# Delta rule: transposes by VectorE's 32x32 turns and a DRAM buffer in place of TensorE's, in a generator of its own

## The chip, the core and the metric

One core of a Trainium2 chip runs the kernel. TensorE (PE, and PEld for its weight loads), VectorE (DVE), ScalarE (ACT), GpSimd (POOL) and SyncE (SP, which here only issues transfers) each work through their own queue in the order in which the program issued. The metric is the device time of one execution in microseconds; a profile's span runs from the first to the last instruction.

## What is computed

One layer of a hybrid decoder for 256 prompt rows and 32 sample rows (8 sequences of 4), width 2048, all in float32. The part that matters here is the gated delta rule with 8 heads of 128:

```python
qkv, new_gdn_buf = causal_depthwise_conv(jnp.concatenate([q, k, v], -1), gdn_buf, gdn_conv_w)
q, k, v = jnp.split(jax.nn.silu(qkv), 3, axis=-1)
qh = l2norm(q.reshape(hs)); kh = l2norm(k.reshape(hs)); vh = v.reshape(hs)
o, S = gated_delta_rule(qh, kh, vh, g, beta, S0)
o = o * lax.rsqrt(jnp.mean(o * o, -1, keepdims=True) + NORM_EPS) * gdn_norm_w
o = o * jax.nn.silu(z.reshape(hs))
y_b = o.reshape(Bsz, L, D_GDN) @ w_b_out
```

with, for each chunk of 64 rows, inside gated_delta_rule:

```python
M = jnp.where(strict, jnp.einsum('nbhid,nbhjd->nbhij', kb, kc) * decay, 0.0)
T = lax.linalg.triangular_solve(eye + M, eye, left_side=True, lower=True, unit_diagonal=True)
u = T @ (vc * bc);  w = T @ (kb * jnp.exp(gcum)[..., None])
...
v_new = u_c - w_c @ S
o = qd @ S + a_c @ v_new
S = S * jnp.exp(gl)[..., None] + jnp.einsum('bhcd,bhce->bhde', kd, v_new)
```

Around it stand the projections: x @ w_in (11280 columns), w_a_out, w_b_out, w_o, and the two feed-forward products with 8192 hidden columns.

## The kernel before

**The main stream.** Every weight is cut into blocks of 512 KB. A block is loaded on SP's queue (`load`, tile raw), split into two float32r halves, hi on ScalarE (`split_hi`) and lo on VectorE (`split_lo`), and used by 24 matmuls (`matmuls`: hi by x's high part, hi by its low part, lo by its high part). The loop at the end of `hybrid_kernel` takes block i in step i; in it the engines get, in this order: `split_hi(i + 3)`, one part of the side work, `split_lo(i + 3)`, the evacuations that are due, the 24 matmuls of block i, and `load(i + 7)`. raw, hi and lo have four buffers each.

**The evacuations.** Four blocks make a group of 256 columns; for keys, queries and values of a half of the heads (two groups each) its convolution comes one step after the group (`conv_evac`, f: two copies and a product on ScalarE, small copies on POOL, three L143 instructions on VectorE), the second 128 columns one step later, and the Silu two steps later. The first half's groups are blocks 0 to 23 (keys, queries, values), the second half's 24 to 47; then come the groups of the short convolution (48 to 95) and z (96 to 111), whose evacuation multiplies into ao, so the delta rule's output has to lie there by then.

**The side work.** `side()` is a generator: gates, then `gdn(0)` and `gdn(1)`, each a half of the heads. A part up to the next `yield` is issued in each step, ahead of the step's matmuls on TensorE's queue. gdn starts in step 20 for the first half. The delta rule needs rows where the projection gives columns (heads' channels on the partitions), and takes them by TensorE transposes against the identity: kq (L958), the sample's kqs (L973, L974, L980), v (L1219) and the output (L1291). For the sample rows four matmuls against a widened Us (L1176) give v_new in another arrangement. `T` and its inverse are built by steps of 8, 16 and 32 (L1084), `states_of` multiplies the sample's keys and queries into S0 (L1072), and a chain over four chunks c does p1 (L1231), p2 (L1243), p3 (L1251) and p4 (L1254). Its first instruction on v scales v by nr, out of PSUM.

**The sample's generator.** `sample()` is a second generator (`aux`); one part of it is issued in each step after the side work. Its first part has sp1 (L1139 to L1142) and Es, its third and fourth the decays of S0 on POOL (L1126), and further ones spread v3 over vm on POOL (L1192), multiply it (pn, L1203) and add to S0.

In the profile, L143 and L140 are the helpers `stt` and `tt`, so one line stands for many operations of VectorE; the tile names tell them apart (lo, w, v, E).

Of the kernel before, what the change touches and what calls it, by code (L numbers as in the profile page):

```python
# [9 lines left out]
F32 = mybir.dt.float32  # L10
# [93 lines left out]
def hybrid_kernel(ctx: ExitStack, tc: tile.TileContext, A):  # L104
# [11 lines left out]
    gp = pool("gp", 4, space=PSUM)  # L116

# [798 lines left out]
    def four(ap):  # L916
        return ap.rearrange("p (h t) -> p h t", h=4).unsqueeze(2).to_broadcast([P, 4, 4, 32])

    def gdn(G):
# [4 lines left out]
        S0 = pl.tile([P, 4, 8, P], F32, tag="S0", name=nm("S0"))  # L924
        for hh in range(4):
            gps.dma_start(S0[:, hh], A["state_gdn"][0, :, 4 * G + hh].rearrange("b d e -> d b e"))

        def T(shape, tag):
            return pl.tile(shape, F32, tag=tag, name=nm(tag))
# [8 lines left out]
        sqr = T([P, 1024], "vmh")  # L938
        rep4 = sqr[:, 512:1024]
        junk = sqr[:, 192:320]  # L940
        wide = rep4.rearrange("p (h q t) -> p h q t", h=4, q=4)
# [5 lines left out]
        gl = T([P, 4, 2, 64], "gl")  # L947
        ss = T([P, 22], "ss")
        red = T([P, 4, 4], "red")
        kdec = T([P, 4, 2, P], "kdec")  # L950
        kst, qst = (kqs[:, u].rearrange("p h b t -> p (h b t)") for u in range(2))
        rows = (slice(0, 64), slice(64, 128))

        for c in range(4):
            kt = gtile()
            kv = kt.rearrange("p (h c) -> p h c", h=4)
            for hh in range(4):
                pe.transpose(kv[:, hh, :], kq[:, hh, c].rearrange("p s x -> p (s x)"), ident)  # L958
            s2 = sqr[:, 512 * (c % 2):512 * (c % 2) + 512].rearrange("p (h c) -> p h c", h=4)
            act.activation(s2, kv, AF.Square)  # L960
            for par in range(2):
                act.copy(kdec[rows[par], c], kv[rows[par], par::2, :])
            dve.tensor_reduce(out=red[:, c, :], in_=s2, axis=mybir.AxisListType.X, op=ADD)
            if c % 2:
# [3 lines left out]
        ssv = ss[:, 0:16].rearrange("p (a c r) -> p a c r", a=2, c=4)  # L968
        for par in range(2):
            act.copy(ssv[rows[par], 0], red[rows[par], :, par::2])  # L970
            act.copy(ssv[rows[par], 1], red[rows[par], :, 1 - par::2])
        sp2 = gtile()
        pe.transpose(sp2[:, 0:128], kst, ident)  # L973
        pe.transpose(sp2[:, 128:256], qst, ident)  # L974

        gps.tensor_copy(wide, four(kst))
        yield
        ktr = gtile()
        for hh in range(4):
            pe.transpose(ktr[:, hh * P:hh * P + P], rep4[:, hh * P:hh * P + P], ident)  # L980
        kr = T([P, 4, P], "kr")
        for u in range(2):
            act.activation(junk, sp2[:, u * P:u * P + P], AF.Square, accum_out=ss[:, 16 + u:17 + u])
        act.copy(kr, ktr.rearrange("p (h d) -> p h d", h=4))
        act.activation(sqr[:, 0:512], ktr, AF.Square)
        dve.tensor_reduce(out=ss[:, 18:22], in_=sqr[:, 0:512].rearrange("p (h d) -> p h d", h=4),
                          axis=mybir.AxisListType.X, op=ADD)
# [6 lines left out]
        yield  # L994
# [26 lines left out]
        kdf = kdec.rearrange("p c r x -> p (c r) x")  # L1021
        tt(kdf, kdf, bc(qc(kdr), P), MUL)
# [21 lines left out]

        Uf, Tf = U.rearrange("p q c -> p (q c)"), Tm.rearrange("p q c -> p (q c)")
# [41 lines left out]
        spread_kq(0)  # L1087
# [48 lines left out]
        def sample():  # L1136
# [32 lines left out]
            act.copy(wide, four(Us))  # L1169
# [4 lines left out]
            vtr = gtile()  # L1174
            for hh in range(4):
                pe.matmul(vtr[:, hh * P:hh * P + P], rep4[:, hh * P:hh * P + P], vs, start=True, stop=True)  # L1176
            vr = sqr[:, 0:512].rearrange("p (h d) -> p h d", h=4)
            tt(vr, vtr.rearrange("p (h d) -> p h d", h=4), bc(rsc[:, 1], P), MUL)
            v3 = pl.tile([P, 4, P], F32R, tag="U", name=nm("v3"))
            lows(v3, vr, 1)  # L1180
            yield
            po = gtile()
# [29 lines left out]
        while cur[0] < mark["kqv_end", G] + 3:  # L1212
            yield
# [241 lines left out]
```

## Time and profile before

| what | us |
|---|---|
| three runs, median | 1707.81 |
| lowest and highest of them | 1706.11, 2056.02 |
| the profiled execution, span from first to last instruction | 1703.4 |
| TensorE busy in it | 1688.5 |
| VectorE, ScalarE, GpSimd busy | 1007.2, 734.1, 133.8 |

No time of the profiled execution other than its span is given; the median of the runs is 4.4 above that span. In the profile's groups, a row has line, engine, operation, output and inputs with their shapes, the count, and then busy time in us, mean of one in ns, and the idle time of the engine just before with what ended it. In the chain and the timeline a row starts with the start and the duration in us, counted from the span's start. Matmuls overlap, so the distance from one start to the next is the price of one, not its duration.

### The profile page before, as it was taken

How to read it: one execution, taken by the hardware profiler on the slowest of the kernel's cores; microseconds unless marked ns; L12 is line 12 of the kernel's file. 1: busy time of each engine (PE TensorE's matmuls, PEld its weight loads, DVE VectorE, ACT ScalarE, POOL GpSimd, SP SyncE). 2: the span in 40 equal slices, each digit the busy share in tenths (PEclk: the TensorE clock that was granted, in tenths of full speed). 3: DMA queues.
4: the chain of work that ended last, by engine and by line, in shares of the span. 5: the costliest groups of instructions: out<-in, count | busy, mean ns of one | idle time of the engine just before them, and what ended most of it. 6: DMA issues, size and time to landing. Idle time of an engine off the chain costs nothing.

```text
span 1703.4 us, 31106 instructions
## 1 busy us (share of the span) xinstructions
PE 1688.5 (99%) x13063; PEld 1668.7 (98%) x13063; DVE 1007.2 (59%) x1296; ACT 734.1 (43%) x1067; POOL 133.8 (8%) x223
## 2 busy tenths in 40 slices
PE   9999999999999999999999999999999999999997
PEld 7999999999999999999999999999999999999997
DVE  5577876758544444456778844566445654466565
ACT  4675626333543333334445533444334433344442
POOL 2232412023300000000010000000000000000000
PEclk9999999999999999999999999999999999999999
DMA  8464456435555555555565555555555555555552
GB/s 244 140 194 139 123 175 200 150 115 180 162 170 169 166 162 170 163 164 165 158 190 174 165 170 161 164 170 162 167 168 161 163 171 162 164 167 164 162 162 80
DMA packets 275097, 279.18 MB, mean 164 GB/s; under 512 B 13131, under 2 KB 270092, under 8 KB 274952
## 3 DMA queue, kind: packets, MB, share of 16 engines
q1 hardware_dynamic: 270414, 265.95, 51.3%
q0 software_dynamic: 4256, 11.12, 2.3%
q8 instruction: 102, 1.67, 0.4%
q14 instruction: 37, 0.30, 0.1%
q10 hardware_dynamic: 288, 0.13, 0.0%
HBM read 269.68 MB, written 7.48 MB: 163 GB/s over the span
## 4 chain that ended last, share of the span: by engine, by line
PE 98%; DVE 1%; DMA 0%; POOL 0%; issue 0%; SPq 0%; ACT 0%; POOLq 0%; ACTq 0%
PE acc L206 31%; PE acc L208 31%; PE acc L207 31%; PE g L1084 1%; DMA xr<-in_x_prompt_dram 0%; PE g L1072 0%; PE g L1231 0%; PE g L1251 0%; PE g L831 0%; DVE w L143 0%; PE g L1254 0%; PE g L1203 0%; PE g L1243 0%; PE g L608 0%; PE g L798 0%; PE g L958 0%
## 5 line engine op out<-in xcount | busy, mean ns | idle before, releaser
L140 DVE TENSOR_TENSOR lo<-raw,hi 128x1024 fp32r<-128x1024 f32 (+2 forms) x502 | 614.0, 1226 | 556.2 <-ACT hi L179 553.7
L179 ACT CAST hi<-raw 128x1024 fp32r<-128x1024 f32 (+1 forms) x498 | 517.6, 1041 | 765.0 <-PE acc L207 707.7
L206 PE MATMUL acc<-xh,hi 128*128 128x288 f32 x1408 | 422.9, 300 | 0.0
L208 PE MATMUL acc<-xh,lo 128*128 128x288 f32 x1408 | 416.7, 296 | 0.0
L207 PE MATMUL acc<-xl,hi 128*128 128x288 f32 x1408 | 416.5, 296 | 0.0
L206 PE MATMUL acc<-dh,hi 128*128 128x290 f32 x1024 | 303.9, 297 | 0.0
L207 PE MATMUL acc<-dl,hi 128*128 128x290 f32 x1024 | 303.3, 296 | 0.0
L208 PE MATMUL acc<-dh,lo 128*128 128x290 f32 x1024 | 302.7, 296 | 0.0
L206 PE MATMUL acc<-hh,hi 128*128 128x288 f32 x1024 | 302.3, 295 | 0.0
L208 PE MATMUL acc<-hh,lo 128*128 128x288 f32 x1024 | 302.3, 295 | 0.0
L207 PE MATMUL acc<-hl,hi 128*128 128x288 f32 x1024 | 302.3, 295 | 0.0
L206 PEld LDWEIGHTS acc<-xh,hi 128*128 128x128 f32 x1408 | 265.4, 189 | 2.6 <-issue 0.7
L207 PEld LDWEIGHTS acc<-xl,hi 128*128 128x128 f32 x1408 | 265.8, 189 | 0.5
L208 PEld LDWEIGHTS acc<-xh,lo 128*128 128x128 f32 x1408 | 265.6, 189 | 0.0
L206 PEld LDWEIGHTS acc<-dh,hi 128*128 128x128 f32 x1024 | 193.6, 189 | 0.1
L208 PEld LDWEIGHTS acc<-dh,lo 128*128 128x128 f32 x1024 | 193.3, 189 | 0.0
L207 PEld LDWEIGHTS acc<-dl,hi 128*128 128x128 f32 x1024 | 193.3, 189 | 0.1
L207 PEld LDWEIGHTS acc<-hl,hi 128*128 128x128 f32 x1024 | 192.5, 188 | 0.0
L208 PEld LDWEIGHTS acc<-hh,lo 128*128 128x128 f32 x1024 | 192.3, 188 | 0.0
L206 PEld LDWEIGHTS acc<-hh,hi 128*128 128x128 f32 x1024 | 192.1, 188 | 0.0
L207 PE MATMUL acc<-ml,hi 128*128 128x288 f32 x256 | 75.6, 295 | 0.0
L208 PE MATMUL acc<-mh,lo 128*128 128x288 f32 x256 | 75.6, 295 | 0.0
(404 smaller groups left out, 1620.0 us busy)
## 6 DMA issues: line engine op xcount, KB each, us to landing
raw<-in_w_in_dram SPq DMA_DIRECT2D x176, 512.0 KB, 3.5
raw<-in_w_up_dram SPq DMA_DIRECT2D x128, 512.0 KB, 3.9
raw<-in_w_down_dram SPq DMA_DIRECT2D x128, 512.0 KB, 3.7
raw<-in_w_o_dram SPq DMA_DIRECT2D x32, 512.0 KB, 3.7
raw<-in_w_a_out_dram SPq DMA_DIRECT2D x16, 512.0 KB, 3.7
raw<-in_w_b_out_dram SPq DMA_DIRECT2D x16, 512.0 KB, 3.6
S<-in_state_gdn_dram POOLq DMA_DIRECT2D x8, 512.0 KB, 7.8
out_dram<-S POOLq DMA_DIRECT2D x8, 512.0 KB, 4.9
```

The costliest lines, as they stand in the source:

```text
L140: dve.tensor_tensor(out=out, in0=a, in1=b, op=op)
L179: act.copy(his[i][:, k:k + step], raw[i][:, k:k + step])
L206: pe.matmul(o, wh, xh_, start=st, stop=False)
L207: pe.matmul(o, wh, xl_, start=False, stop=False)
L208: pe.matmul(o, wl, xh_, start=False, stop=en)
L1084: pe.matmul(out[r, q * 64:q * 64 + 64], a[r, q, :], b[r, q, :], start=True, stop=True)
```

## The change

It touches five things.

1. A pool in DRAM (`dp`) and turns of 32x32 blocks on VectorE take the place of TensorE's transposes. Each is a `dve.transpose`, a write of its 32-row bands to DRAM and a read back in the other arrangement, all on SP's queue: keys and queries (dk), the sample's (ds), v (dv) and the output (do, read straight into ao).
2. What had been the start of gdn is a generator of its own, `prepare(G)`: it is put on a new list `ahead` in step 19 for the first half, and at the end of the first half's `sample()` for the second. One part of it is issued in a step, after `side()` and only when `aux` is empty. gdn(G) starts when prepare(G) has put its tiles into `front`.
3. v is turned and loaded inside gdn, long before its use, and the scaling by nr is one VectorE instruction from SBUF to SBUF, directly ahead of the first p2.
4. The sample's four matmuls against the widened Us are gone: pv goes to DRAM (dx) and comes back as v4. The spread of v3 starts in the same part as v3.
5. S0 shares its tile with the turned keys and queries, so its loads on POOL come after mx; in the chain over chunks every p2 has two parts ahead of its p3, and p3 one ahead of the next p1, in both halves.

```diff
+    def prepare(G):
...
+        for hh in range(4):
+            dve.transpose(out=tk[:, :, hh % 2, :, hh // 2],
+                          in_=kq[:, hh].rearrange("p c s x -> p c (s x)").rearrange("p c (j b) -> p j c b", j=4))
+            if hh == 1:
+                dve.transpose(out=ts.rearrange("p u h x -> p (u h x)"), in_=kqs.rearrange("p u h b t -> p (u h b t)"))
+            if hh == 1:
+                yield
+        ds = dp.tile([8, 32, P], F32, tag="ds", name=nm("ds"))
+        for i in range(4):
+            sp.dma_start(ds[:, :, rows32(i)].rearrange("h b x -> b h x"), ts[rows32(i)].rearrange("p u h x -> p (u h) x"))
+        yield
+        dk = dp.tile([P, 4, 2, 256], F32, tag="dk", name=nm("dk"))
+        for i in range(4):
+            sp.dma_start(dk[:, i].rearrange("(j b) a t -> b j (a t)", j=4),
+                         tk[rows32(i)].rearrange("p j a c r x -> p j (a c r x)"))
+        sp.dma_start(spk, ds.rearrange("(u h) b d -> (h b) u d", u=2))
...
+        yield
+        for a in range(2):
+            r = rows[a]
+            sp.dma_start(kT[r].rearrange("p i c r x -> p i (c r x)"), dk[r, :, a])
+            sp.dma_start(qT[r].rearrange("p i c r x -> p i (c r x)"), dk[r, :, 1 - a])
+        for q in range(4):
+            sp.dma_start(kr[rows32(q)], ds[0:4].rearrange("h b d -> b h d"))
+        yield
...
+        yield
+        yield
+        for u, t in enumerate((kT, qT)):
...
+        yield
...
+        front[G] = (sqr, ss, kT, tv, spk, kr, glx)
     def gdn(G):
...
-            for hh in range(4):
-                pe.transpose(kv[:, hh, :], kq[:, hh, c].rearrange("p s x -> p (s x)"), ident)
...
-        pe.transpose(sp2[:, 0:128], kst, ident)
-        pe.transpose(sp2[:, 128:256], qst, ident)
...
-            pe.transpose(ktr[:, hh * P:hh * P + P], rep4[:, hh * P:hh * P + P], ident)
...
+        while cur[0] < mark["kqv_end", G] + 3:
+            yield
+        for r in range(2):
+            dve.transpose(out=tv[:, :, :, r],
+                          in_=vf[:, r].rearrange("p c a x -> p c (a x)").rearrange("p c (j b) -> p j c b", j=4))
+        yield
...
+            sp.dma_start(dv[:, i].rearrange("(j b) t -> b j t", j=4),
+                         tv[rows32(i)].rearrange("p j c r x -> p j (c r x)"))
+        yield
+        sp.dma_start(v.rearrange("p i c r x -> p i (c r x)"), dv.rearrange("p i t -> p (i t)").rearrange("p (i t) -> p i t", i=4))
...
         act.copy(mx[:, 0], Xf)
         gps.tensor_tensor(out=mx[:, 1], in0=Xf, in1=mx[:, 0], op=SUB)
+        S0 = T([P, 4, 8, P], "S0")
+        for hh in range(4):
+            gps.dma_start(S0[:, hh], A["state_gdn"][0, :, 4 * G + hh].rearrange("b d e -> d b e"))
         yield
+        spread_kq(0)
         yield
...
             pe.matmul(pv_[:, 0:P], Us, vs, start=True, stop=True)
+            act.copy(Xs, pv_[:, 0:P])
             act.mul(vns, pv_[:, 0:P], sc[:, 1:2])
-            for hh in range(4):
-                pe.matmul(vtr[:, hh * P:hh * P + P], rep4[:, hh * P:hh * P + P], vs, start=True, stop=True)
...
+            yield
+            sp.dma_start(dx, Xs)
...
             done.append(1)
+            yield
+            for q in range(4):
+                sp.dma_start(v4[rows32(q)], dx.rearrange("(h b) d -> b h d", h=4))
+            yield
+            yield
+            vr = sqr[:, 0:512].rearrange("p (h d) -> p h d", h=4)
+            tt(vr, v4, bc(rsc[:, 1], P), MUL)
+            v3 = pl.tile([P, 4, P], F32R, tag="U", name=nm("v3"))
+            lows(v3, vr, 1)
...
             store(3)
+            if G == 0:
+                ahead.append(prepare(1))
...
         aux.append(sample())
-        v = T([P, 4, 2, P], "v")
-        for u in range(2):
-            vt = gtile()
-            for w in range(4):
-                pe.transpose(vt[:, w * P:(w + 1) * P], vf[:, w % 2, 2 * u + w // 2].rearrange("p a x -> p (a x)"), ident)
-            tt(v[:, 2 * u:2 * u + 2].rearrange("p c r x -> p (c r) x"), vt.rearrange("p (q x) -> p q x", q=4),
-               bc(nr[:, 4 * u:4 * u + 4], P), MUL)
-        yield
+        yield
+        vq = v.rearrange("p i c r x -> p i (c r) x")
+        tt(vq, vq, bc(bmid(nr[:, 0:8], 4), 32), MUL)
...
             p2 = gtile()
             for p in range(2):
-                pe.matmul(p2[:, p * P:(p + 1) * P], U128[:, 2 * c + p, :], v[:, c, p, :], start=True, stop=True)
+                pe.matmul(ix(p2[:, p * P:(p + 1) * P]), U128[:, 2 * c + p, :], v[:, :, c, p], start=True, stop=True)
...
-            if c == 0 or G == 0:
-                yield
+            yield
...
-            if G == 0:
-                yield
...
+        to = T([P, 4, 2, 4, 32], "kdec")
+        for r in range(2):
+            dve.transpose(out=to[:, :, r], in_=o[:, :, r].rearrange("p c (j b) -> p j c b", j=4))
+        yield
+        do = dp.tile([2, 2, P, 2, 4, 32], F32, tag="do", name=nm("do"))
+        for i in range(4):
+            sp.dma_start(do[1 - i // 2, i % 2].rearrange("(j b) r c x -> b j (r c x)", j=4),
+                         to[rows32(i)].rearrange("p j r c x -> p j (r c x)"))
+        yield
+        for a in range(2):
+            for r in range(2):
+                t0 = gd["ao"][:, 1, 4 * G + a + 2 * r, 0:NP_].rearrange("p (c n x) -> p n c x", c=4, n=2)
+                for n in range(2):
+                    sp.dma_start(t0[:, n], do[a, n, :, r])
         yield
...
         for G in range(2):
-            while cur[0] < mark["kqv", G] + 20 or aux:
+            while G not in front or aux:
                 yield
...
+                if i == mark["kqv", 0] + 19:
+                    ahead.append(prepare(0))
                 next(sgen, None)
                 if aux and next(aux[0], aux) is aux:
                     aux.pop(0)
+                if ahead and not aux and next(ahead[0], ahead) is ahead:
+                    ahead.pop(0)
```

More of the change, by code (lines that the diff above doesn't have):

```diff
@@ L913, in gates, with rows32, T @@
         yield
-    def four(ap):
-        return ap.rearrange("p (h t) -> p h t", h=4).unsqueeze(2).to_broadcast([P, 4, 4, 32])
-    def gdn(G):
+    def rows32(n):
+        return slice(32 * n, 32 * n + 32)
+    def T(shape, tag, bufs=1):
+        return gd["pool"].tile(shape, F32, tag=tag, name=nm(tag), bufs=bufs)
+    rows = (slice(0, 64), slice(64, 128))
+    front = {}
+    def prepare(G):
         pl = gd["pool"]
-        hs = slice(4 * G, 4 * G + 4)
         pr = slice(2 * G, 2 * G + 2)
-        kq, kqs, vf, vfs = gd["kq", G], gd["kqs", G], gd["v", G], gd["vs", G]
-        S0 = pl.tile([P, 4, 8, P], F32, tag="S0", name=nm("S0"))
-        for hh in range(4):
-            gps.dma_start(S0[:, hh], A["state_gdn"][0, :, 4 * G + hh].rearrange("b d e -> d b e"))
-        def T(shape, tag):
-            return pl.tile(shape, F32, tag=tag, name=nm(tag))
-        def qc(ap):
-            return ap.rearrange("p c r -> p (c r)")
-        b4 = T([P, 1152], "b4")
-        Es, Ts, Xs, nMs, aTs, Us, vs, vns, junk2 = (b4[:, P * u:P * u + P] for u in range(9))
-        kqm = b4.rearrange("p (a x) -> p a x", a=2)
[L938 to L941, printed above, removed]
-        U128 = T([P, 8, P], "U128")
-        aT = T([P, 8, P], "aT")
-        gps.memset(kqm, 0.0)
-        for z in (U128, aT):
-            gps.memset(z, 0.0)
[L947 to L956, printed above, removed]
-            for hh in range(4):
[L958 to L964, printed above, removed]
-                yield
@@ L994, in gdn, with qc @@
         yield
+        for u, t in enumerate((kT, qT)):
+            s2 = sqr.rearrange("p (q i x) -> p i q x", q=8, i=4)
+            act.activation(s2, t.rearrange("p i c r x -> p i (c r) x"), AF.Square)
+            dve.tensor_reduce(out=ss[:, 8 * u:8 * u + 8], in_=sqr.rearrange("p (q d) -> p q d", q=8),
+                              axis=mybir.AxisListType.X, op=ADD)
+        yield
+        for u in range(2):
+            act.activation(junk, spk[:, u], AF.Square, accum_out=ss[:, 16 + u:17 + u])
+        act.activation(sqr[:, 0:512], kr.rearrange("p h d -> p (h d)"), AF.Square)
+        dve.tensor_reduce(out=ss[:, 18:22], in_=sqr[:, 0:512].rearrange("p (h d) -> p h d", h=4),
+                          axis=mybir.AxisListType.X, op=ADD)
+        front[G] = (sqr, ss, kT, tv, spk, kr, glx)
+    def gdn(G):
+        pl = gd["pool"]
+        hs = slice(4 * G, 4 * G + 4)
+        pr = slice(2 * G, 2 * G + 2)
+        kq, kqs, vf, vfs = gd["kq", G], gd["kqs", G], gd["v", G], gd["vs", G]
+        sqr, ss, kT, tv, spk, kr, glx = front[G]
+        v4 = sqr[:, 512:1024].rearrange("p (h d) -> p h d", h=4)
+        def qc(ap):
+            return ap.rearrange("p c r -> p (c r)")
+        b4 = T([P, 1152], "b4")
+        Es, Ts, Xs, nMs, aTs, Us, vs, vns, junk2 = (b4[:, P * u:P * u + P] for u in range(9))
+        kqm = b4.rearrange("p (a x) -> p a x", a=2)
+        U128 = T([P, 8, P], "U128")
+        aT = T([P, 8, P], "aT")
+        gps.memset(kqm, 0.0)
+        for z in (U128, aT):
+            gps.memset(z, 0.0)
+        kdec = T([P, 4, 2, P], "kdec")
+        kst, qst = (kqs[:, u].rearrange("p h b t -> p (h b t)") for u in range(2))
         gr = gtile()
```

67 lines of the change are left out of this document (29 added, 38 removed).

## The prediction

> **What bounds the kernel now.** I read the page's first part (who is busy), its fourth part (the chain that ended last), then who waited for whom, then the chain in order of time around the delta rule.
>
> ```profile
> PE 1688.5 (99%) x13063; PEld 1668.7 (98%) x13063; DVE 1007.2 (59%) x1296; ACT 734.1 (43%) x1067; POOL 133.8 (8%) x223
> ...
> PE 98%; DVE 1%; DMA 0%; POOL 0%; issue 0%; SPq 0%; ACT 0%; POOLq 0%; ACTq 0%
> ...
> L179 ACT CAST hi<-raw 128x1024 fp32r<-128x1024 f32 (+1 forms) x498 | 517.6, 1041 | 765.0 <-PE acc L207 707.7
> ```
>
> TensorE is the bound: 99% busy, 98% of the chain. ScalarE's copy of a weight block waits for TensorE (707.7 of 765.0 us), not for a transfer, so the weight stream runs ahead. So only two things move the time: instructions taken off TensorE's queue, and waits that come or go in that queue. The only long wait inside the span, and its weaker twin in the second half of the heads, are these (waits view, then chain):
>
> ```profile
> PE g L1203 <- DVE E L143: 3.0, 1, 3.0
> ```
> ```profile
> 405.38 0.61 DVE E L143 x2
> ```
>
> **What comes off TensorE.** The chain in order of time gives each kind of removed work; the row of L973 (L974 is equal) is from the groups by form:
>
> ```profile
> 92.99 0.87 PE g L958 x8
> 97.06 0.87 PE g L958 x8
> 104.53 0.44 PE g L980 x4
> ...
> 180.11 0.87 PE g L1219 x8
> 184.95 0.61 PE g L1243 x4
> ...
> 201.15 0.89 PE g L1176 x8
> ...
> 271.72 0.87 PE g L1291 x8
> ...
> 366.19 0.87 PE g L1219 x8
> 371.03 0.44 PE g L1243 x4
> ```
> ```profile
> L973 PE MATMUL g<-cf,kqs 128*128 128x128 f32 x2 | 0.5, 272 | 0.0
> ```
>
> A step without other work is 97.06 - 92.99 - 0.87 = 3.20 us, so the 0.87 is fully added to its step. Per half of the heads the change drops 16 key/query transposes (2 x 0.87), 8 of v (0.87), 8 of the output (0.87), 4 of L980 (0.44), 2 of L973/L974 (2 x 0.87/8 = 0.22) and the 8 passes of L1176 (0.89): 5.03. Both halves: **-10.1 us**. The matmuls that stay (L1243, L1251, L1254) read v in four runs of 32 columns instead of one of 128; no row shows such a read, I take the same price; bounds: nothing, and a doubling of L1243's 0.44 in its 8 uses (+3.5).
>
> **What VectorE and the rest pay.** Turning adds, per half, 8 instructions of 128x512 and one of half that:
>
> ```profile
> L1114 DVE STREAM_TRANSPOSE xt<-U x4: 711/712/712, 155.9 to 352.8; 128x512 f32<-128x512 f32 x4
> ```
> ```profile
> 92.70:439.40 346.70, 343.63 (x3054) 335.69 (x3053) 253.15 (x407) 175.88 (x338) 82.95 (x121) 1.00 0.52 156
> ```
>
> That is 8 x 0.71 + 0.4 = 6.1 us. The reductions before (five a half) become three of like total. VectorE is 253.15 of 346.70 us busy here (73%), so 6 us in some 130 us find room; ScalarE loses the copies out of PSUM. By themselves these cost nothing: a block's halves are ready three steps (9.6 us) ahead. If that cover goes, the price is where TensorE waits for a VectorE result in the same step; that is the main item below.
>
> **The transfers.** Weights and the new round trips share SP's queue:
>
> ```profile
> raw<-in_w_in_dram SPq DMA_DIRECT2D x176, 512.0 KB, 3.5
> ...
> ao<-in_w_in_dram SPq DMA_DIRECT2D x1, 128.0 KB, 5.9
> ```
>
> SP waits for each turn on VectorE, and for each write before its read; the weight load of that step is queued behind. Write and read are one step apart (3.2 us) against some 3.5 us landing, so SP loses a microsecond or two. The worst burst is the eight loads of a half's output into ao: 8 x 128 x 4 = 4096 pieces of 128 B. The nearest row moved 2048 pieces of 64 B in 5.9 us, so 4096 take at most 11.8. Load i+7 leaves about 2.5 us into step i (after hi 1.04 and lo 1.2) and must be split by step i+7: 22.4 - 2.5 - 3.5 - 2.3 = 14 us of room. Cost taken: zero; bounds 0 and 5 (burst, issues and a late write together). The Trainium skill ("DMA: Bandwidth & Descriptors", Specifications) says that pieces below 512 B fall short of line rate through a read-modify-write; this speaks against the change, and the 5.9 us row is in its favour. By that rule the burst is longer than its bytes ask for, which the 11.8 us from the row already allows.
>
> Every other step that moves (S0's loads on POOL from the start of gdn to after mx, six steps ahead of states_of; v's turn; dx and v4 with two steps between load and use) has at least two steps (6.4 us) before its user: zero. The second half's front starts when the first half's sample is stored, and its first turn waits for that store on VectorE; TensorE needs nothing of it for 8 steps: zero.
>
> **The new wait.** Before, v was scaled by nr one step ahead of the first matmul on it (p2, L1243). Now the scaling is issued in the same step as p2, directly ahead of it, behind all that VectorE has from the step before. Counting the yields: prepare(0) runs in steps 19 to 26, gdn(0) starts at 27, U128 and the first part of sample are step 45, the scaling and p2 step 46. Before, they were steps 42 and 43. The same VectorE and ScalarE work, both halves:
>
> ```profile
> 367.04 1.24 ACT L1121 COPY U<-U 64x512 f32<-64x512 f32 x2
> ...
> 368.55 0.35 ACT L1145 ACTIVATE b<-g,nr 128x128 f32<-128x128 f32 x1
> ```
> ```profile
> 368.93 0.35 DVE L143 SCALAR_TENSOR_TENSOR b<-g,sc,b 128x128 f32<-128x128 f32 x1 [0.63 <-ACT b L1145]
> ...
> 370.10 0.31 DVE L1151 STREAM_TRANSPOSE b<-b 128x128 f32<-128x128 f32 x1
> 370.34 1.18 DVE L140 TENSOR_TENSOR lo<-raw,hi 128x1024 fp32r<-128x1024 f32 x1
> ```
> ```profile
> L140 DVE TENSOR_TENSOR kdec<-kdec,kdr 128x1024 f32<-128x1024 f32 x2 | 2.4, 1215 | 0.0
> ```
>
> Second half: VectorE is through with the step's lo at 371.5; the scaling (128x1024, like kdec's, 1.22) ends at 372.7. TensorE reaches p2 at 371.03 less the 0.87 of the removed transposes, 370.16. **+2.6 us** of wait.
>
> First half: the same, plus a table load on ScalarE, plus a convolution piece (three instructions of L143 for the value columns, blocks 40 to 43, due in steps 44 and 45), and POOL's four decays of S0. These are issued in steps 47 and 48, but POOL has nothing queued ahead of them after step 45's small copies, so it runs them early, as it did before:
>
> ```profile
> 182.22 1.28 ACT L1144 ACT_TABLE_LOAD   x1
> ```
> ```profile
> 174.01 1.70 DVE L143 SCALAR_TENSOR_TENSOR w<-w,hw 128x312 f32<-128x312 f32 x3 [0.61 <-ACT w L270]
> ...
> 179.24 4.89 DVE L143 SCALAR_TENSOR_TENSOR w<-w,hw 128x312 f32<-128x312 f32 x3
> 184.04 1.28 DVE L140 TENSOR_TENSOR v<-g,nr 128x512 f32<-128x512 f32 x2
> ```
> ```profile
> 178.19 5.01 POOL L1126 TENSOR_TENSOR S<-S,gexp 128x1024 f32<-128x1024 f32 x2
> ```
> ```profile
> 345.30 3.79 POOL L1126 TENSOR_TENSOR S<-S,gexp 128x1024 f32<-128x1024 f32 x2
> ```
>
> Beside two decays the three took 4.89 us instead of 1.70, and the decays 5.01 instead of 3.79: the two engines take turns. Set the step's side work at 180.11 as in the row: TensorE reaches p2 at 184.95 - 0.87 = 184.1. ScalarE's table load ends 183.5, Exp and the copy of vs 184.1, VectorE's chain takes to 185.6 (as 368.9 to 370.4). Without POOL: lo 1.2, three of L143 1.7, scaling 1.2, end 189.7: a wait of 5.6. With POOL: the four decays start about 184.9, after the piece's copies, and now nothing stands between the second and the third; 4 x 1.9 = 7.6 of decays and 4.1 of VectorE in turn end at 196.6: a wait of 12.5. Before, only two decays came at this place. I take **+12.5**, nearest to the 179.24 row, bounds 5.6 and 13.
>
> The Trainium skill ("SBUF — State Buffer", Who interferes with whom) has it as an exclusive lock: a VectorE instruction with two SBUF inputs and a POOL instruction that reads SBUF block each other for a whole instruction. If instead both only slowed (factor 4.89/1.70 for L143, less for the others), the scaling would end about two microseconds earlier, a wait near 10.5; the rows (5.01 and 4.89 interleaved) are nearer to turns.
>
> **Old waits.** The 3.0 us came from POOL's spread meeting the last value pieces (steps 49, 50). The spread now comes in step 54, where no such piece runs: -3.0. The 0.61 is a PSUM buffer that the sample's product wants while p3 still holds it; p3 and the first product now meet in both halves (steps 56 and 97): 2 x 0.61 - 0.61 = +0.6; bounds 0 and 3.
>
> **Sum.** -10.1 - 3.0 + 12.5 + 2.6 + 0.6 = +2.6 us on a span of 1703.4: 1706.0. The runs' median 1707.81 is 4.4 above the span (lowest 1706.11: 2.7), start and end around it; I keep that 4.4 and get **1710 us**. Bounds of the pieces: 5.6 in place of 12.5 gives 1703; all upper ends (13, 3, 5, 3.5) give 1722.
>
> **Rivals.** *Faster, the waits are hidden:* VectorE reaches the scaling before TensorE reaches p2. Then -10.1 - 3.0 + 0.6 = -12.5: 1695. For it: in the 184.04 row v was ready just in time though VectorE was late. Against: there it had a step (4 us) more. It decides if VectorE is less than half a microsecond behind; a partial form with POOL out of the way (5.6 + 2.6) gives 1703. *Slower, the output burst starves the weights:* if 128 B pieces take 11.8 us and land only after the 14 us of room, TensorE stands in both halves; from 14 us on each further one costs two. At 20 us: 2.6 + 12 = +15, 1722. Against: the 5.9 us row is an upper bound already. *The change does not take TensorE's time off* (strided reads doubling): +3.5, 1714.
>
> **Chances.** Both waits about as worked out (1706 to 1715): 0.55; partly hidden (1699 to 1706): 0.17; hidden (under 1699): 0.13; burst or strided reads (over 1715): 0.15. The range leaves out half of the last two: 1697 to 1720; the likeliest alone is 1706 to 1715. Two per cent (34 us) is about what a measurement of this kernel can tell from none: faster would need three times the removed work (0.01), slower 45 us of new stalls (0.02), the rest within (0.97).
>
> **What would show it.** Right: no L958, L980, L1176, L1219, L1291 kinds left on TensorE; in the waits view TensorE waiting for v, once near 12 us around 184 + 3 and once near 3 us; four decays in one row on POOL there, L143 at 1.6 us each beside them. Wrong: no wait of TensorE for v; or waits of lo for hi, and hi for raw, after either half's output; or L1243 longer than 0.44 per four.

## The result, and the profile after

| | before | after |
|---|---|---|
| median of the runs | 1707.3 us | 1727.5 us (1726.7 to 1729.0, 4 runs) |
| ratio | 1 | 1.0121, 95% interval 1.0105 to 1.0136 |
| span of the profiled execution | 1703.4 us | 1724.7 us |

The kernel became slower by about 20 us, 1.2%. The forecast was 1710, its range ended at 1720. One of the four runs before took 2056.02 us and is left out of the ratio. In the changed file most lines stand one to forty lower: the weights' third matmul L208 is L209, the helpers `tt` and `stt` are L141 and L144, the split's hi is L180, p2 is L1277, the solve's pairs are L1113, POOL's decays L1158, and the copy of X that ScalarE makes in the solve is L1140.

The page of the changed kernel, its first, fourth and fifth part:

```profile
PE 1687.5 (98%) x12971; PEld 1666.1 (97%) x12971; DVE 1018.4 (59%) x1308; ACT 722.7 (42%) x1028; POOL 133.5 (8%) x221
...
PE 90%; DVE 5%; DMA 2%; issue 1%; ACT 1%; SPq 1%; POOLq 0%; POOL 0%; DVEq 0%; ACTq 0%
...
L180 ACT CAST hi<-raw 128x1024 fp32r<-128x1024 f32 (+1 forms) x498 | 517.4, 1041 | 786.5 <-PE acc L208 710.4
```

Busy time hardly tells anything: TensorE issues 92 instructions fewer and is busy 1 us less. The chain tells: TensorE had 98% of it, now 90%, and VectorE, DMA and SP's queue are on it. The waits (engine and line that waits, what it waits for; us in all, times, longest us) name the places; the second fence is ScalarE's own list:

```profile
PE g L1277 <- DVE v L141: 14.6, 2, 11.8
PE acc L209 <- DVE lo L141: 6.3, 2, 5.0
PE g L1113 <- ACT xt L1140: 3.9, 2, 2.3
...
PE g L1239 <- DVE E L144: 0.8, 2, 0.6
```
```profile
ACT hi L180 <- DMA raw<-in_w_in_dram: 30.7, 10, 8.1
```

The first row is the forecast wait for v: 11.8 and 2.8 us against 12.5 and 2.6. Its making is the forecast one too (timeline of POOL, then VectorE; start, duration, row):

```profile
195.76 8.90 POOL L1158 TENSOR_TENSOR S<-S,gexp 128x1024 f32<-128x1024 f32 x4
```
```profile
198.20 2.58 DVE L141 TENSOR_TENSOR lo<-raw,hi 128x1024 fp32r<-128x1024 f32 x1
200.70 4.87 DVE L144 SCALAR_TENSOR_TENSOR w<-w,hw 128x312 f32<-128x312 f32 x3
205.49 1.22 DVE L141 TENSOR_TENSOR v<-v,nr 128x1024 f32<-128x1024 f32 x1
```

Four decays in one row, a lo of 2.58 us and three convolution pieces of 4.87 us beside them; the scaling that p2 needs comes last, after POOL is done, at its plain 1.22 us.

The next two rows were not forecast. The last one was: the sample's product (L1239) wants a PSUM buffer that VectorE still adds to the state (tile E), 0.8 us in two places, where this view of the kernel before has none and +0.6 was the term. And the four longest waits (2.3, 11.8, 5.0 and 2.8 us) cost more than their length. In these windows, one behind each of them, of the changed kernel the columns after the length are busy us (count) of PE, PEld, DVE, ACT, POOL, then the granted clock, the DMA share and GB/s:

```profile
163.50:165.90 2.40, 2.40 (x38) 2.28 (x40) 1.11 (x2) 0.89 (x1) 0.00 (x0) 0.51 0.98 236
```
```profile
207.80:211.30 3.50, 3.50 (x16) 3.50 (x16) 1.82 (x3) 0.00 (x0) 0.00 (x0) 0.50 0.12 18
...
301.20:306.40 5.20, 5.20 (x22) 5.20 (x22) 2.34 (x5) 2.25 (x4) 0.00 (x0) 0.50 1.01 295
```
```profile
382.70:385.30 2.60, 2.60 (x12) 2.60 (x12) 1.82 (x3) 0.00 (x0) 0.00 (x0) 0.50 0.36 128
```

Behind each of the four long waits TensorE runs at half the clock. The matmuls come 0.24 us apart there, and 0.13 us apart as soon as the clock is back:

```profile
210.59 0.44 PE L209 MATMUL acc<-xh,lo 128*128 128x288 f32 x1
210.84 0.44 PE L207 MATMUL acc<-xh,hi 128*128 128x288 f32 x1
...
211.45 0.29 PE L207 MATMUL acc<-xh,hi 128*128 128x288 f32 x1
211.58 0.29 PE L208 MATMUL acc<-xl,hi 128*128 128x288 f32 x1
```

At 0.133 us each the 16, 22 and 12 matmuls of the last three windows would take 2.1, 2.9 and 1.6 us: 1.4 + 2.3 + 1.0 lost. The first window's two groups, L1113 and L1101, took 1.97 and 2.70 us, where the same groups before the change took 1.15 and 1.97: 1.55 lost. That is 6.2 us for the clock alone, an estimate from these rows.

So the miss (the span forecast 1706.0, come 1724.7: 18.7 us) is put together from: wait for v -0.5, wait for lo +6.3, wait for the X copy (xt) +3.9, clock +6.2, the PSUM buffer (E) +0.2: 16.1. The remaining 2.6 us have no name.

### The profile page after: what moved, and what is told of

The parts are those of the page before. It is cut to its first block, busy times and chain, and to the rows that moved or that the text cites. A ratio compares the mean times of both kernels' runs of the same rounds, so it can differ in the third digit from the quotient of the medians.

```text
span 1724.7 us, 31034 instructions
## 1 busy us (share of the span) xinstructions
PE 1687.5 (98%) x12971; PEld 1666.1 (97%) x12971; DVE 1018.4 (59%) x1308; ACT 722.7 (42%) x1028; POOL 133.5 (8%) x221
## 4 chain that ended last, share of the span: by engine, by line
PE 90%; DVE 5%; DMA 2%; issue 1%; ACT 1%; SPq 1%; POOLq 0%; POOL 0%; DVEq 0%; ACTq 0%
PE acc L207 29%; PE acc L208 29%; PE acc L209 29%; DVE lo L141 2%; DMA raw<-in_w_in_dram 1%; DVE w L144 1%; PE g L1113 1%; PE g L1101 0%; ACT hi L180 0%; DMA out_dram<-S 0%; PE g L799 0%; PE g L1265 0%; DMA xr<-in_x_prompt_dram 0%; PE g L1277 0%; PE g L832 0%
## 5 line engine op out<-in xcount | busy, mean ns | idle before, releaser
L141 DVE TENSOR_TENSOR lo<-raw,hi 128x1024 fp32r<-128x1024 f32 (+2 forms) x502 | 614.7, 1228 | 550.1 <-ACT hi L180 547.9
L180 ACT CAST hi<-raw 128x1024 fp32r<-128x1024 f32 (+1 forms) x498 | 517.4, 1041 | 786.5 <-PE acc L208 710.4
L209 PE MATMUL acc<-xh,lo 128*128 128x288 f32 x1408 | 419.3, 298 | 6.3 <-DVE lo L141 6.3
L208 PE MATMUL acc<-xl,hi 128*128 128x288 f32 x1408 | 418.8, 297 | 0.0
L208 PE MATMUL acc<-dl,hi 128*128 128x290 f32 x1024 | 303.3, 296 | 0.0
L209 PE MATMUL acc<-dh,lo 128*128 128x290 f32 x1024 | 302.7, 296 | 0.0
L208 PE MATMUL acc<-hl,hi 128*128 128x288 f32 x1024 | 302.3, 295 | 0.0
L209 PE MATMUL acc<-hh,lo 128*128 128x288 f32 x1024 | 302.3, 295 | 0.0
L209 PEld LDWEIGHTS acc<-xh,lo 128*128 128x128 f32 x1408 | 267.8, 190 | 6.8 <-DVE lo L141 6.8
L208 PEld LDWEIGHTS acc<-xl,hi 128*128 128x128 f32 x1408 | 268.1, 190 | 0.5
L209 PEld LDWEIGHTS acc<-dh,lo 128*128 128x128 f32 x1024 | 193.3, 189 | 0.0
L208 PEld LDWEIGHTS acc<-dl,hi 128*128 128x128 f32 x1024 | 193.3, 189 | 0.1
L208 PEld LDWEIGHTS acc<-hl,hi 128*128 128x128 f32 x1024 | 192.5, 188 | 0.0
L209 PEld LDWEIGHTS acc<-hh,lo 128*128 128x128 f32 x1024 | 192.3, 188 | 0.0
L208 PE MATMUL acc<-ml,hi 128*128 128x288 f32 x256 | 75.6, 295 | 0.0
L209 PE MATMUL acc<-mh,lo 128*128 128x288 f32 x256 | 75.6, 295 | 0.0
```

The lines of the kernel that those rows point to most:

```text
L141: dve.tensor_tensor(out=out, in0=a, in1=b, op=op)
L180: act.copy(his[i][:, k:k + step], raw[i][:, k:k + step])
L208: pe.matmul(o, wh, xl_, start=False, stop=False)
L209: pe.matmul(o, wl, xh_, start=False, stop=en)
```

## The experiments

Each run's edit is against the changed kernel, its ratio against the kernel before. A time from four runs is known to some 2.6 us (half the width of its interval), one from ten to some 1.6; where an edit gains less, the waits of its trace carry the argument and not the time.

**Is the wait for v the decays' and the place of the scaling?** e1 moves the scaling ahead of the solve's last round; e2 moves the decays four steps on and leaves the scaling.

```diff
         for s in (8, 16, 32):
+            if s == 32:
+                tt(vq, vq, bc(bmid(nr[:, 0:8], 4), 32), MUL)
             px = gtile()
```

> Only the scaling of v by nr is moved, three parts earlier (into the step of the last px, ahead of it), so that it no longer stands in the step of the first p2. Theory (TensorE stands at the first p2 because VectorE reaches the scaling late, and then runs some microseconds at half clock): the two waits of L1277 for v (11.8 and 2.8 us) go, and with them the slow matmuls right behind them (some 2 us together): about 17 us less than the changed kernel, 1710 us. Rival (VectorE's lag, not the scaling, is the limit and shows at the next product that needs it): another wait of TensorE on VectorE of 5 us or more appears within a few steps, and the time stays over 1718 us.

1716.6 us (1714.1 to 1718.0), ratio 1.0062 [1.0047, 1.0077]: 10.9 us back where the theory had 17. The wait for v at p2 is gone; a new one, under the rival's 5 us, came at p3, one step on, where VectorE's lag behind the decays now shows:

```profile
PE g L1286 <- DVE v L141: 3.8, 1, 3.8
```

```diff
             yield
-            for hh in range(2):
-                decay(hh)
             pxs = gtile()
...
+            for hh in range(2):
+                decay(hh)
             dx = dp.tile([P, P], F32, tag="dx", name=nm("dx"))
...
```

> Only POOL's four decays of S0 are issued four parts later, behind the last value columns' convolution. Theory (VectorE's instructions with two SBUF inputs take turns with POOL's decays): in the first half the three convolution instructions ahead of the scaling fall from 4.9 to 1.7 us and the wait of the first p2 from 11.8 to about 5.5 us; the second half's 2.8 us stays; 1721 us. Rival (VectorE is late there because of the work itself or of ScalarE's table load, and POOL does not matter): the wait stays over 10 us, 1727 us.

1724.0 us (1722.7 to 1724.3), ratio 1.0105 [1.0090, 1.0120]: the first wait fell from 11.8 to 5.7 us, with POOL out of the way. VectorE's rows at the same place:

```profile
198.19 1.18 DVE L141 TENSOR_TENSOR lo<-raw,hi 128x1024 fp32r<-128x1024 f32 x1
199.30 1.69 DVE L144 SCALAR_TENSOR_TENSOR w<-w,hw 128x312 f32<-128x312 f32 x3
200.91 1.22 DVE L141 TENSOR_TENSOR v<-v,nr 128x1024 f32<-128x1024 f32 x1
```

1.18 and 1.69 us in place of 2.58 and 4.87: these 4.6 us go with POOL's decays. The wait is near the forecast's lower bound, 5.6, and the changed kernel's 11.8 near its 12.5. Of the 6.1 us only 3.5 came back in time, since other waits grew (lo from 6.3 to 7.4, E from 0.8 to 1.7).

**What makes lo late at the second half's front?** At 275 to 300 us the second half's front and the first half's output share SP's queue and the 16 DMA engines with the weights. SP's timeline of the changed kernel:

```profile
277.73 0.39 SPq L172 DMA_DIRECT2D raw<-in_w_in_dram  x1
278.17 3.37 SPq L956 DMA_DIRECT2D dk<-S  x4
281.65 1.17 SPq L958 DMA_DIRECT2D kso<-ds  x1
282.94 1.02 SPq L172 DMA_DIRECT2D raw<-in_w_in_dram  x1
284.00 4.50 SPq L1324 DMA_DIRECT2D do<-kdec  x4
...
293.40 0.39 SPq L172 DMA_DIRECT2D raw<-in_w_in_dram  x1
293.87 6.58 SPq L1331 DMA_DIRECT2D ao<-do  x8
300.56 9.32 SPq L172 DMA_DIRECT2D raw<-in_w_in_dram  x5
```

Three weight loads in 22 us, where a step takes 3.2. It looks like a queue that issues too late. e5 gives all these transfers to POOL's queue:

```diff
 def prepare(G):
+        qu = gps if G else sp
...
-            sp.dma_start(ds[:, :, rows32(i)].rearrange("h b x -> b h x"), ts[rows32(i)].rearrange("p u h x -> p (u h) x"))
+            qu.dma_start(ds[:, :, rows32(i)].rearrange("h b x -> b h x"), ts[rows32(i)].rearrange("p u h x -> p (u h) x"))
```

> All transfers of the second half's front (ds, dk, kso, kT/qT, kr) and the first half's output (do, ao) are issued by POOL's queue; SP keeps the weights there. Theory order (SP issues the weights late, because 21 issues of about 0.5 us and their waits stand ahead of them in its queue): TensorE's waits for lo (6.3 us) and the half clock behind them (2.4 us) go, about 1719 us. Theory supply (the 16 DMA engines are full: 5.7 us of busy share in 275 to 300 us at only 213 GB/s, as the pieces are small): the weights are as late from any queue, lo wait 4 to 8 us, 1725 to 1732 us.

1726.2 us (1723.3 to 1728.5), ratio 1.0115 [1.0099, 1.0131]; wait for lo 6.2 us. SP's queue held weights alone, and lo was as late. SP's timeline of e5, then its windows:

```profile
275.13 37.11 SPq L172 DMA_DIRECT2D raw<-in_w_in_dram  x10
```
```profile
285.00:290.00 5.00, 5.00 (x40) 5.00 (x39) 2.28 (x2) 1.21 (x2) 3.10 (x6) 1.00 1.02 332
290.00:295.00 5.00, 5.00 (x39) 4.91 (x38) 0.00 (x0) 1.05 (x1) 2.11 (x4) 1.00 1.08 253
295.00:300.00 5.00, 1.72 (x13) 1.48 (x12) 1.22 (x1) 1.69 (x2) 3.15 (x5) 1.00 1.09 240
```

The DMA share is full at 240 to 332 GB/s: the order of issue is not the cause, and the full DMA engines are what is left. But what TensorE stands for is not the weight block itself. ScalarE's rows of the changed kernel, then VectorE's:

```profile
290.14 1.05 ACT L180 CAST hi<-raw 128x1024 fp32r<-128x1024 f32 x1 [6.23 <-DMA raw<-in_w_in_dram]
295.33 1.06 ACT L977 ACTIVATE vmh<-S 128x1024 f32<-128x1024 f32 x1 [4.14 <-DMA S<-dk]
```
```profile
296.43 1.22 DVE L978 TENSOR_REDUCE ss<-vmh 128x8 f32<-128x1024 f32 x1 [9.74 <-ACT vmh L977]
...
299.90 1.21 DVE L141 TENSOR_TENSOR lo<-raw,hi 128x1024 fp32r<-128x1024 f32 x1
```

The block's raw came late, but its hi was done at 291.2 and VectorE was idle. The lo of this block stood in VectorE's queue behind L978, the sums of squares that prepare(1) takes of keys and queries. L978 waited 9.74 us for the squares on ScalarE (L977), and these for the front's own read, S<-dk. Lo ran from 299.90, and TensorE went on at 301.2. In e5 the same two lines wait 9.29 and 5.11 us, the block's hi is done at 291.9, its lo starts at 301.6, and the next hi finds its raw already there: lo is late although the weights have come.

VectorE's stand at these sums and TensorE's wait for lo right behind it go together in all runs: 9.2 to 9.7 us with 4.4 to 6.2 (changed, e1 to e7, e9), 8.7 with 2.1 (e8), 7.1 to 8.3 with 1.1 to 3.2 (e10, e11, e13, e15, e16), 5.0 to 5.7 with none (e12, e14, e17). At the first half's front VectorE stands 2.5 us, and TensorE does not wait. No run moved the sums alone, so what the late weights would cost without them stays open. The second wait for lo, 1.4 us at 320 us, stands behind 13 us of VectorE's own work without a pause.

e4 spreads the first half's eight reads of ao over eight steps behind the front.

```diff
+        def into_ao():
...
                     for n in range(2):
                         sp.dma_start(t0[:, n], do[a, n, :, r])
+                        yield
+        if G == 0:
+            ahead.append(into_ao())
```

> Only the first half's eight reads of the output into ao are issued one a step after the second half's front, instead of eight in one step beside it. Theory (their 128-byte pieces, together with the front's own 2 MB, keep the weight blocks from coming): the waits of TensorE for lo (5.0 and 1.3 us) and the half-clock stretch behind them go, about 9 us less, 1718 us. Rival (the front's write and read of keys and queries alone hold the weights up): the wait for lo stays over 4 us, and the time over 1724 us.

1726.9 us (1726.4 to 1730.4), ratio 1.0130 [1.0113, 1.0147]: the second wait for lo went, the first stayed (4.7 us), and the waits for the X copy grew from 3.9 to 6.2 us, most of it in the second half, where the last of the spread reads (327 and 328 us) lie beside S0's loads (from 327 us). Nothing gained.

e7 makes them one read of 1 KB pieces.

```diff
-                for n in range(2):
-                    sp.dma_start(t0[:, n], do[a, n, :, r])
+        ta = T([P, 2, 2, 2, 4, 32], "v")
+        sp.dma_start(ta.rearrange("p a n r c x -> p (a n) (r c x)"), do.rearrange("a n p r c x -> p (a n) (r c x)"))
...
+                gps.tensor_copy(t0, ta[:, a, :, r])
```

> The output's read from the DRAM buffer goes in one transfer of 1 KB pieces into v's tile, and POOL spreads it into ao by four copies, in place of eight transfers that leave pieces of 128 B. Theory small pieces (packets under 512 B fill the DMA engines at 290 to 305 us): packets under 512 B between 270 and 305 us fall from 5704 to under 1600, the busy share in 293 to 300 us from 1.25 to under 1, TensorE's waits for lo from 6.3 to under 3 us, 1721 to 1724 us. Rival (dk's and do's bulk decides): packets fall, waits stay over 5 us, 1726 us or more.

1723.5 us (1721.3 to 1725.2), ratio 1.0099 [1.0084, 1.0114]. Packets under 512 B between 270 and 310 us fell from 5751 to 1552, but one wait for lo of 4.6 us stayed, and the DMA share at 295 to 300 us is still 1.14. The 4 us gained are in the range; "under 3 us of waiting" and a share under 1 were not met. The wait at the front's sums is hardly shorter (4.6 for 5.0 us); what went is the second wait for lo.

e8 gives the output back to TensorE, with the lines of the kernel before (L1286 to L1295 there).

> Both halves' output is turned by TensorE again (16 transposes, 1.7 us in all), so do and ao's 1 MB written and read are gone; front, v and sample stay as changed. If the meeting of output and second front is the cause: TensorE's waits for lo are under 1.5 us in all, and the time is 1727.5 - 6.3 - 2.4 + 1.7 + up to 1, about 1720 us. If the second half's front alone holds the weights up: waits for lo 4 us or more, 1726 to 1729 us.

1723.7 us (1723.3 to 1725.9), ratio 1.0106 [1.0089, 1.0122], 3.8 us gained where 7.5 were expected. Wait for lo 2.1 us, between the two forecasts: without the output's transfers the front still makes a wait here, a third of it. VectorE stands 8.7 us at the front's sums instead of 9.7, and the second wait for lo is gone.

**What makes the X copy late?** Either the weights' late arrival on ScalarE's queue (hi waits for raw, X copy behind it), or ScalarE's other work. S0's loads (2 MB a half) were moved in the change next to v's turn.

```diff
-        for hh in range(4):
-            gps.dma_start(S0[:, hh], A["state_gdn"][0, :, 4 * G + hh].rearrange("b d e -> d b e"))
...
+        s0_load(0)
         yield
         spread_kq(0)
+        s0_load(1)
         yield
...
```

> Only S0's four loads are spread over steps 34, 35, 37 and 38 instead of one step. Theory (2 MB of S0 in one go hold up the weight blocks, hi waits, the copy of X behind it on ScalarE is late, and TensorE waits at the pq of size 8): the waits of L1113 for xt (2.3 and 1.6 us, and what stands beside them) shrink to under 1 us in total; about 5 us less, 1722 us. Rival (ScalarE is late there because VectorE's convolution is): the waits stay near 4 us, 1727 us.

1727.3 us, ratio 1.0122 [1.0107, 1.0137]; waits for the X copy 3.8 us, as before. Spreading over four neighbouring steps does nothing. e6 turns v in its own tile, which frees S0's tile earlier, and loads S0 much earlier.

```diff
-        tv = flat[:, 0:1024].rearrange("p (j c r x) -> p j c r x", j=4, c=4, r=2)
...
+        tv = v.rearrange("p i c r x -> p (i c r x)").rearrange("p (j c r x) -> p j c r x", j=4, c=4, r=2)
...
+        def slot(n):
+            hh = n - 3 * G
+            if 0 <= hh < 4:
+                gps.dma_start(S0[:, hh], A["state_gdn"][0, :, 4 * G + hh].rearrange("b d e -> d b e"))
```

> v is turned in its own tile, so S0's four loads of 512 KB can go one a step from the step of aT on (about 130 to 140 us in the first half, 324 to 335 us in the second), before and not beside v's read, mx and the solve's start. Theory supply: the waits for the X copy (xt, 3.9 us in two places, 0.7 and 1.6 us longer steps beside) shrink to under 1.5 us and the time is 1722 to 1725 us. Rival (the X copy is late because ScalarE's own work before it is long, not because hi waits for raw): the waits stay near 4 us, 1727 us.

1726.4 us (1724.0 to 1727.6), ratio 1.0115 [1.0100, 1.0130]. The gain of 1.1 us is not clear of the noise; by the waits both theories hold, one in each half. In the second half the wait is gone. In the first it stays at 2.1 us, though the DMA engines had nothing to hold up there: share 0.35 in e6's window, where the changed kernel had 1.06. ScalarE's timeline of e6 shows its queue waiting on VectorE ahead of the copy:

```profile
155.00:160.00 5.00, 5.00 (x62) 4.77 (x62) 4.89 (x8) 0.00 (x0) 0.00 (x0) 1.00 1.06 321
```
```profile
158.24 0.42 ACT L286 ACTIVATE kq<-w 128x256 f32<-128x256 f32 x1 [4.04 <-DVE w L144]
...
160.99 0.42 ACT L286 ACTIVATE kq<-w 128x256 f32<-128x256 f32 x1 [2.21 <-DVE w L144]
...
162.37 0.57 ACT L1151 COPY xt<-g 128x512 f32<-128x512 f32 x1
```

VectorE is late with w because the solve's 17 small operations (first and last row below, from e6; 5.0 us in a row) now stand among these convolution pieces. Before the change the first of them came at 141.22:

```profile
150.51 0.19 DVE L1139 COPY vmh<-cf 128x64 f32<-128x64 f32 x1
...
154.78 0.71 DVE L1145 STREAM_TRANSPOSE xt<-U 128x512 f32<-128x512 f32 x1
```
```profile
141.22 0.20 DVE L1096 COPY vmh<-cf 128x64 f32<-128x64 f32 x1
```

e10 takes v's turn with its transfers and scaling, and S0's loads, out of the delta rule's generator into ones that run beside it.

```diff
+        para.extend((s0_loads(), v_turn()))
         yield
         yield
-        while cur[0] < mark["kqv_end", G] + 3:
-            yield
-        for r in range(2):
-            dve.transpose(out=tv[:, :, :, r],
...
+        while not vok:
+            yield
```

> v's turn and scaling and S0's loads go in generators beside the delta rule, so its solve starts three steps (9.6 us) earlier, where it started before the change; decays and output stay as changed. Theory place in the step order (in the first half the X copy waits behind ScalarE's kq activations, which wait for VectorE's w; VectorE is behind because the solve's 4.9 us of small operations stand three steps later than before the change): the first half's X copy wait (2.3 us) and its 7 us step go back to 3.1 us. The wait for v's scaling goes, a lag of the decays at p3 (about 4 us) may stay: 1710 to 1716 us. Rival (supply alone makes the X copy late): the step at 160 us stays at 6 us or more.

1717.7 us (1717.0 to 1719.0), ratio 1.0066 [1.0051, 1.0081]. In the step of the X copy the time between the weights' matmuls is 3.07 us again (7.03 changed), as the place theory has it. The solve's first products start at 140.5 instead of 146.0 us, two steps earlier, not the three of the expectation. But new waits came: for mx (2.9 for ScalarE's part, 2.2 for POOL's), lo 2.8, v 2.9 and the sample's b 2.5, so the time lies above the range.

**Do the gains add?** e9 puts e1, e2, e6 and e7 together; e11 is e10 with e2 and e7, e12 is e10 with e2 and e8.

> Four single edits together: v scaled early, decays later, S0's loads early, output read in 1 KB pieces. If the waits are separate causes their gains add: from 1727.5, the early scaling -10.9 and the wait of p3 that it left (3.8, from the same decays) -3.8, output -4, S0 -1 to -3.6: 1705 to 1709 us. If the waits only trade places (TensorE waits for the same late engine somewhere else): above 1713 us.

1706.4 us (1704.2 to 1707.9, 10 runs), ratio 0.9998 [0.9989, 1.0008], inside the range: the single gains are 10.9 + 3.5 + 1.1 + 4.0 = 19.5, the joint one 21.1, the same within the noise. No wait for v is left over 0.2 us. What is:

```profile
PE acc L209 <- DVE lo L141: 5.1, 2, 4.8
PE g L1125 <- ACT xt L1154: 2.1, 1, 2.1
...
PE g L1253 <- DVE E L144: 1.7, 2, 1.5
```

> As e10, with the decays later and the output read in 1 KB pieces. If the named waits (v, lo, xt) are all that the change put on TensorE, then what is left is the removed work (-10.1), the removed wait (-3.0) and at most one wait for lo of 3 us: 1694 to 1703 us, ahead of 1706.6 before. If turning by VectorE and DRAM has a cost besides these waits: 1704 us or more.

1710.7 us (1709.2 to 1714.3, 8 runs), ratio 1.0028 [1.0017, 1.0038]: missed. The wait for the X copy is gone; waits for mx (2.2 + 2.2), lo 2.4, E 1.9 and the sample's product 2.4 came in its place.

> As e11, but both halves' output is turned by TensorE (+1.7 us) and its 1 MB written and read is gone, so that only the second half's front competes with the weights at 275 to 300 us. If the meeting of front and output makes the wait for lo: no wait over 1 us, 1696 to 1700 us, under e11 when e11 keeps a wait for lo. If the front alone does: about e11 + 1.7.

1708.4 us (1706.7 to 1710.5, 10 runs), ratio 1.0010 [1.0001, 1.0019]: the wait for lo is 0.5, and it lies at 139 us, not at the second half's front, but the other waits keep the time 8 us above the range. With e11's wait of 2.4 us at the front gone, this is for the meeting. In e14 and e17, too, the front alone makes no wait, in e8, e13 and e16 it does; why its read lands in time in the one order and not in the other was not taken apart. The solve's new place trades waits.

**The meeting of front and output, with the rest quiet.** e13 is e9 with e8 in place of e7; e14 is e13 with the first half's solve as early as in e10, and e15 is e14 with e7 in place of e8.

> As e9, but both halves' output is turned by TensorE (+1.7 us), so that the second half's front meets no output. If the meeting makes most of the wait for lo (e9: 5.1 us, and about 2 us of half clock behind it), at most 2.2 us are left and the time is 1706.4 - 3 - 2 + 1.7 = 1702 to 1704 us. If the front alone makes it: wait 4 us or more, 1707 to 1709 us.

1704.3 us (1703.0 to 1705.9, 10 runs), ratio 0.9986 [0.9977, 0.9995]: ahead of the kernel before by 2 us. Wait for lo 3.0 us in three pieces, 1.1 of it at the front's sums and 1.6 at 303 us behind VectorE's own work, where e9 had 5.1; in all a little more than "at most 2.2". What e14 has in another way than e10:

```diff
-            while cur[0] < mark["kqv_end", G] + 3:
+            while cur[0] < mark["kqv_end", G] + 5:
...
-        yield
-        yield
+        for _ in range(2 + 2 * G):
+            yield
```

> As e13, but in the first half the solve starts three steps earlier (where it stood before the change), with v's turn two steps behind it in a generator beside; the second half keeps the order of the change. Theory place: the first half's wait for the X copy (2.1 us in e9, step of 6.8 us) goes back to a step of 3.1 us, and the time is e13 - 3.7 = 1698 to 1701 us, if no other wait of the solve comes (mx, E). Rival (transfers make it late): step over 6 us, time as e13.

1709.0 us (1707.7 to 1712.0, 10 runs), ratio 1.0014 [1.0004, 1.0024]. The step of the X copy has 3.07 us between the weights' matmuls (e13: 6.83), so place holds; the time is 4.7 above e13 all the same, since TensorE now waits for E in other places, 4.6 and 1.9 us.

> As e14, but with the output by VectorE's turn and one read of 1 KB pieces, as in e9. Difference to e14 is the meeting of front and output: wait for lo 2 to 5 us and its half clock, less 1.7 us of TensorE's turns: e14 + 1 to + 4 us.

1709.9 us (1707.6 to 1713.4, 10 runs), ratio 1.0022 [1.0012, 1.0031]: e14 + 1, which is not clear of the noise, with a wait for lo of 3.5 us against 0.2. Once more front and output meeting; without TensorE's turns it costs about what they do.

**Are the last waits the decays'?** e16 is e13, and e17 is e14, with each decay alone beside the solve.

```diff
             act.copy(X, px.rearrange("p (q c) -> p q c", c=64))
+            if s > 8:
+                decay(s // 8 - 2)
             yield
...
+            else:
+                decay(s // 8 - 1)
             yield
```

> As e13, with each decay issued alone, two beside the solve's step s=16 and two beside s=32, ahead of the sample part. Theory turns (decays on POOL lengthen VectorE's operations beside them, and the one that TensorE waits for is whichever is late there): the waits for E (1.7 us) fall under 0.5 us; the X copy's step at 162 us stays near 6.8 us; 1702 to 1704 us. Rival (the solve's VectorE operations are then the late ones): waits in the solve (Tm, U, X) of 1 us or more a decay, 1706 to 1712 us.

1702.9 us (1701.0 to 1704.5, 10 runs), ratio 0.9979 [0.9969, 0.9988]: the fastest of all, 3.6 us ahead of the kernel before. E fell from 1.7 to 0.8, not under the 0.5 of the expectation.

> As e14, with the decays placed as in e16. Theory turns: the waits for E (4.6 and 1.9 us) fall under 1 us in all, 1701 to 1703 us. Rival (the chain waits for E because VectorE has more work beside it in this order, whatever POOL does): waits for E of 4 us or more stay, 1707 to 1709 us.

1706.7 us (1705.9 to 1708.1, 10 runs), ratio 1.0002 [0.9992, 1.0011]: the 1.9 is gone, the 4.6 stays. The rival's number came for that one, and VectorE's rows, then POOL's, say what stands ahead of E:

```profile
384.20 2.01 DVE L332 TENSOR_SCALAR w<-w,hwa 128x304 f32<-128x304 f32 x1
386.25 2.62 DVE L144 SCALAR_TENSOR_TENSOR w<-w,hwa,w 128x304 f32<-128x304 f32 x2
388.79 0.36 DVE L332 TENSOR_SCALAR w<-w,hwa 128x304 f32<-128x304 f32 x1
389.19 1.11 DVE L144 SCALAR_TENSOR_TENSOR w<-w,hwa,w 128x304 f32<-128x304 f32 x2
```
```profile
383.23 2.81 POOL L1245 TENSOR_TENSOR vm<-v,cf 128x1024 fp32r<-128x1024 f32 x1 [2.38 <-DVE v L144]
```

The same two convolution rows take 2.01 and 2.62 us beside POOL's spreads of vm and 0.36 and 1.11 without, so POOL has a part in it that the rival left out. It looks like the old wait of the kernel before (3.0 us for E, with POOL's spread of vm beside the convolution), come back by another order; no run moved this spread alone.

## Why the prediction was wrong

- *What comes off TensorE, -10.1; old wait, -3.0; PSUM, +0.6.* The old wait is gone and the PSUM buffer costs 0.8. With nearly all other costs taken out, the best kernel that keeps the turning of the front and of v (e16) is 3.6 us ahead of the kernel before, with 6.1 us of waits left (lo 3.2, xt 2.1, E 0.8) and 1.7 us of turns on TensorE. 3.6 + 6.1 + 1.7 = 11.4 of the 13.1 are there; the rest was not taken apart.
- *The new wait, +12.5 and +2.6.* Right: 11.8 and 2.8 (14.6 against 15.1). e1 removes it by place alone, e2 brings it to the lower bound by POOL alone. The exclusive lock that the Trainium skill states ("SBUF — State Buffer", Who interferes with whom) agrees with the rows: 4.87 us with the decays and 1.69 without, for the same three instructions. 11.8 lies between the forecast by turns, 12.5, and the one by mere slowing, 10.5, and nearer to the first.
- *The transfers, zero.* This is the step that failed most. The prediction looked for a burst of 11.8 us at the end of a half and gave weights 14 us of room; it did so for each transfer by itself. Of the second half's front it said "TensorE needs nothing of it for 8 steps: zero". TensorE does not, but ScalarE and VectorE do: their squares and sums (L977, L978) stand in their queues ahead of the next weight halves. In the first half's last steps front, output and weights run together for 25 us with the DMA engines full (e5), the front's read lands late, VectorE stands 9.7 us at the sums, and lo comes 5.0 us too late for TensorE. That is most of the 6.3 us, and 2.3 us of half clock follow. The prediction had the cover right (halves ready three steps, 9.6 us, ahead) and saw nothing that would use it up. Its named sign came in part: hi waited 6.2 us for raw, but lo stood behind the sums and not behind hi. The rival "output burst starves the weights" is the nearest to it; it had the burst alone, in both halves, and 1722. The second half's output met no front and made no wait.
- *S0's loads and "every other step that moves", zero.* Failed too, by 3.9 us: with v's turn and the weights they made ScalarE's queue late in the second half (e6), and in the first half the extra steps of v's turn moved the solve among other work of VectorE's (e10, e14). The prediction asked whether each result is in time for its own user; the X copy, like lo, was late because of what stood ahead of it in an in-order queue.
- *A wait costs its length.* Not said, but in the sum: 6.2 us of half clock behind the waits were missing. The 3.0 us wait in the trace of before gave no hint, as the window behind it has the full clock (row below).
- *Strided reads of v, zero.* Right: four p2 matmuls of the changed kernel, which read v in four runs, take what L1243 took in the forecast's row (371.03, 0.44 us):

```profile
415.33 0.44 PE g L1277 x4
```

## What to carry to other kernels

A result that TensorE needs much later can still stop it: ask which instruction on any engine waits for it first, and what stands behind that instruction in the same queue. Add up what all queues move in one stretch before costing a single transfer at zero. Work put into a step-ordered generator shifts everything behind it against the work of the other engines, so the steps added are a cost to look at, whatever they hold. And a wait on TensorE can cost more than its length: here some 6.2 us of half clock came on four waits of 21.9 us together.

## What the runs showed of the hardware

The granted clock fell to 0.50 after waits of 11.8, 5.0, 2.8 and even 2.3 us, for 2 to 5 us; but the kernel before waited 3.0 us at the same kind of place and kept the full clock:

```profile
215.00:217.00 2.00, 0.21 (x1) 0.21 (x2) 1.97 (x7) 0.54 (x2) 0.00 (x0) 1.00 0.72 214
217.00:219.00 2.00, 2.00 (x16) 1.96 (x16) 2.00 (x4) 0.00 (x0) 1.56 (x1) 1.00 0.14 49
```

In e6 it fell to 0.50 after a wait of 2.1 us, and in e4 it stayed at 1.00 after one of 2.9. So length alone does not decide. The Trainium skill ("TensorE: Matmul & The Clock Gate", Part 1: The HAM clock gate) states one idle window of about 3.4 us for the drop, and that the window runs free. The waits of 2.3 and 2.8 us are shorter than this window and yet dropped it; that a wait of 3.0 us once drops nothing would fit windows that run free, but no run here was made to show it.

Full DMA engines did not always move the same: in e5's windows 332 GB/s at a share of 1.02 and 253 at 1.08. The share counts 16 engines, and values over 1 stand in several windows, so it says that they are full but not by how much.
